# A depthwise convolution's product slots, laid token by token instead of slot by slot

## The chip, the cores and the metric

The kernel runs on one core of a Trainium2 chip. The metric is the device time of one execution in microseconds (us). The core's engines work side by side, each through a queue of its own in order: TensorE (PE; its weight loads are PEld), VectorE (DVE), ScalarE (ACT), GpSimd (POOL) and SyncE (SP, which issues the loads of weights).

## What is computed

The reference is a small decoder of two layers over 256 tokens of 2048 features: a Conformer convolution, an MLP, one shared K and V, an attention layer, a second MLP and a final norm. The change touches only the convolution of the first layer:

```python
def conformer_conv(y, w_in, b_in, w_dw, b_dw, ln_g, ln_b, w_out, b_out):
    u = y @ w_in + b_in
    a, gate = jnp.split(u, 2, axis=-1)
    u = a * jax.nn.sigmoid(gate)
    u = lax.conv_general_dilated(
        u, w_dw[:, None, :], window_strides=(1,), padding=[(CONV_WIDTH - 1, 0)],
        dimension_numbers=("NWC", "WIO", "NWC"), feature_group_count=u.shape[-1]) + b_dw
    u = jax.nn.silu(layernorm(u, ln_g, ln_b))
    return u @ w_out + b_out
```

The convolution is depthwise: each of the 2048 features has 31 taps of its own, and an output token is the sum of 31 products of a tap with an earlier token of the same feature.

## The kernel before

Activations lie with features on the 128 partitions and the 256 tokens along the free dimension, so 2048 features are 16 feature tiles, c = 0 to 15. Weights come in chunks of 1 MB (`raw`). Nearly every chunk is split into `hi` (a cast on ScalarE, L138) and `lo` (a subtraction, L140, on GpSimd for the chunks of this stage and on VectorE later), and a product runs as three matmuls per K tile (L193 to L195), 48 for a chunk. Eight chunks of the first product run unsplit as plain float32 (L199).

The stage of the change is a loop over the feature tiles. For tile c, TensorE makes the two halves `pa` and `pg` of the first product; ScalarE makes the sigmoid (L396), and VectorE multiplies both into `u` (L397), a tile of 30 zeros and 256 tokens, of which there are two in turn. Then `conv(c, u)` does the 31 taps:

- ScalarE makes 14 products, each the 256 tokens from a shifted start times one tap per partition (L303), into slots of two `prod` tiles of 8 slots by 256 tokens, float32, three buffers in turn.
- GpSimd adds one slot to another in the first tile and two to two in the second (L311), which frees three slots; ScalarE refills them with the last three of its 14 products.
- VectorE makes two running sums over the other 17 taps in PSUM (L324, L327, L329). Their last steps write slots 0 and 1 of the first `prod` tile.
- VectorE reduces the 8 slots of the first tile into slot 0 of the second (L335, 2048 words to 256), and the 6 slots of the second into the result `v` (L335, 1536 words to 256).

Tile 15 differs: TensorE takes 18 of its taps as products with diagonals (made on ScalarE at L413 during tile 11), and there is one reduction only. A slot is 256 contiguous words, so that the slots of one token lie 256 words, 1 KiB, apart. A tile's mean enters TensorE two tiles later (L418). From tile 12 on VectorE subtracts a provisional mean (L361) and ScalarE squares (L363); when all tiles are done, the LayerNorm's statistics follow and the second product begins.

The order on each engine is set by a scheduler that takes the program's order and priorities (`u` and its sigmoid have a high one) and estimates of its own, so edits can move instructions.

Of the kernel before, what the change touches and what calls it, by code (L numbers as in the profile page):

```python
# [11 lines left out]
F32 = mybir.dt.float32  # L12
# [9 lines left out]
KT = D // P          # feature tiles of the residual stream  # L22
# [7 lines left out]
FQ = 4               # quarters of the MLP's hidden layer  # L30
# [4 lines left out]
# Columns of the packed per-feature vectors: 16 feature tiles each.  # L35
# [5 lines left out]
LOOK = 4             # weight chunks split ahead of the one in use  # L41
RAWS = 3             # weight chunks on their way or waiting to be split
N0 = 4               # output tiles of a product that starts while its operand is still being made
LAST = 13            # K tiles before this one run for all of those

# The first mixer. Its products and its depthwise convolution keep every engine busy, so:
S1_PLAIN = {0, 1, 2, 3, 4, 5, 11, 28}   # chunks of its first product that run as float32
POOL_LO = (set(range(36)) - {28}) | set(range(183, 202, 2))   # chunks (here and in the attention) that GpSimd splits
SLOTS = 8            # partial sums of the convolution that one reduction adds up
# Per reduction: taps that ScalarE multiplies, and how many of them GpSimd adds to others, which makes  # L50
# room for as many more.
PIECES = [(6, 1), (5, 2)]
PE_TAPS = {15: (18, [(6, 1)])}   # feature tiles with taps on the tensor engine: how many, and their PIECES
DIAGS = {11: [15]}   # during which tile those taps' diagonals are made
Y_SPLIT = {0: 2, 1: 9, 2: 16}   # operand tiles that are split by the end of a feature tile
SHIFT = 10           # feature tiles whose mean is the LayerNorm's provisional one
CENTER = {12: [0, 3, 7], 13: [1, 2, 5, 6], 14: [4, 12, 13], 15: [8, 9, 10, 11, 14, 15]}   # when tiles are centered
AHEAD = {13: 31, 14: 34, 15: 34}   # chunks split after a feature tile's gate, where not the next tiles'
# [3 lines left out]
def decoder_kernel(ctx, tc, xT, vec, rope, mask, w_in, w_out, w_k, w_v, w_q, w_o, m_in, m_out, out):  # L62
    """Activations lie feature-major: tile k of a [2048, 256] activation holds features
    128k..128k+127 on the partitions and the 256 tokens along the free dimension. A weight chunk
    [128, 16, 128] holds all of K for 128 output features, so one PSUM tile [128, 256] accumulates
    over its 16 K tiles.

    float32 products: both operands are split exactly, v = hi + lo, hi = v rounded to float32r's 12
    significant bits and lo = v - hi (which has 12 at most), and x.w = xh.wh + xl.wh + xh.wl, each an
    exact one-pass product that is summed in float32. What is left, xl.wl, is below float32's last  # L70
    place of x.w. Attention's own products and a part of the first one, where the vector engine is
    short of time, run as plain float32.
    """
# [30 lines left out]
    def load():  # L104
        """Load as many chunks as there is room for. Those that are not split take a split one's place."""
        while len(raws) < min(len(order), n_used[0] + LOOK + RAWS):
            i = len(raws)
            src, split = order[i]
            if live[split] == ROOM[split]:
                break  # L110
            live[split] += 1
            raw = wp.tile([P, D], F32, name="raw", tag="w")
            if i == 0:
                for j in range(2):
                    nc.sync.dma_start(out=raw[:, j * D // 2:(j + 1) * D // 2], in_=src[:, j * D // 2:(j + 1) * D // 2])
                    nc.sync.dma_start(out=h[:, 4 * j + 4:4 * j + 8, :], in_=xT[:, 4 * j + 4:4 * j + 8, :])
            else:
                nc.sync.dma_start(out=raw, in_=src)
            raws.append(raw)
# [5 lines left out]
    def split_upto(n):  # L125
        """Make the chunks before the n-th ready for use."""
# [60 lines left out]
    def product(ps, w, acts, ks):  # L187
        """ps += the chunk's 128 output features over the K tiles ks."""
# [19 lines left out]
    def scaled_split(f, gain):  # L208
        """hi and lo of tile f of the residual stream times a gain vector."""
# [8 lines left out]
    def col_sums(st, s, first, last):  # L218
        """st[:, b] += a feature tile's part of the mean over features, tokens of half b on the partitions."""
# [9 lines left out]
    def spread(pb, rc):  # L229
        """A per-token column [128, 2] along every partition: [128, 256]."""  # L230
# [3 lines left out]
    class Rms:  # L234
        """The inverse root mean square per token of the residual stream, from tiles as they come."""
# [13 lines left out]
        def columns(self):  # L249
            """[tokens of a half, half]"""  # L250
# [8 lines left out]
        def rows(self):  # L259
            """The same along every partition."""  # L260
# [7 lines left out]
    with ExitStack() as s1:  # L268
# [16 lines left out]
        def conv(c, u):  # L285
            """Depthwise convolution: VectorE's two running sums and ScalarE's products (some added up by
            GpSimd), added up in reductions; the tensor engine may take taps as products with a diagonal."""
# [12 lines left out]
            def scaled(buf, slots):  # L300
                nonlocal j
                for i in slots:
                    nc.scalar.activation(out=buf[:, i, :], in_=u[:, j:j + T], func=AF.Copy, scale=tap(c, j))  # L303
                    j += 1

            for n, m in pieces:
                buf = prodp.tile([P, SLOTS, T], F32, name="prod")
                scaled(buf, range(carry, carry + n))
                if m:
                    room = slice(carry + m, carry + 2 * m)  # L310
                    nc.gpsimd.tensor_tensor(out=buf[:, carry:carry + m, :], in0=buf[:, carry:carry + m, :],  # L311
                                            in1=buf[:, room, :], op=ALU.add)
# [5 lines left out]
            # The running sums are in PSUM: with both inputs in SBUF, VectorE would shut GpSimd out of it.  # L318
            last = bufs[0][0]
            for i, j in enumerate(range(j, TAPS)):  # L320
# [7 lines left out]
                else:  # L328
                    nc.vector.scalar_tensor_tensor(out=a if j < TAPS - 2 else last[:, i % 2, :], in0=x,  # L329
# [3 lines left out]
            for i, (buf, n) in enumerate(bufs):  # L333
                dst = bufs[i + 1][0][:, 0, :] if i + 1 < len(bufs) else v_of(c)
                nc.vector.tensor_reduce(out=dst, in_=buf[:, :n, :].rearrange("p j t -> p t j"), axis=AX.X, op=ALU.add)  # L335
# [23 lines left out]
        def center(c):  # L359
            """Take the provisional mean from tile c, and square it."""  # L360
# [5 lines left out]
        def statistics():  # L366
            """Add the tiles centered so far to the statistics. (What the provisional mean leaves of the
            tiles that it is of sums to nothing.)"""
# [57 lines left out]
        # LayerNorm over the channels. With v less the provisional mean, the mean that is left has a  # L426
        # square of at most (KT - SHIFT) / KT of the mean square, so the difference is a safe variance.
# [52 lines left out]
    def project(acts, add, gain, steps, last):  # L480
        """The first N0 output tiles run together, K tile by K tile as the steps give them (a step may
        also be a function to call), because the operand is still being made. The K tiles from last on
        go output tile by output tile, so that the next chunk need not wait for all of them."""
# [71 lines left out]
    def rotate(src):  # L555
        """Rotary embedding of the first 32 rows of a [128, 256] head, in place."""
# [43 lines left out]

# [1 line left out]
    # The three branches see subsets of the causal keys with the same scores, and are mixed by the  # L602
    # softmax of their log-sum-exps: that is one softmax in which a key counts as often as branches
    # see it. The mask holds the logarithm of that count. Heads go in pairs that share K and V.
# [3 lines left out]
    def scores(p):  # L608
        """Scores and softmax of a pair: queries on the partitions, keys along the free dimension."""
# [29 lines left out]
    def flip(p):  # L639
        """Softmax weights with the keys on the partitions."""  # L640
# [12 lines left out]
    def mix(p):  # L653
        """The pair's outputs, feature-major and split."""
# [53 lines left out]
def rope_rows():  # L708
    """[32, 2, 256]: cosines and signed sines of the rotated rows, by position."""
# [6 lines left out]
def branch_counts():  # L716
    """[128, 2, 256]: for query 128b+p and each key, the log of how many branches see it."""
# [10 lines left out]
def chunks(w):  # L728
    """[K, N] -> [N/128, 128, K/128 * 128]: for each tile of output features, K by partition."""
# [38 lines left out]
```

## Time and profile before

| what | value |
|---|---|
| time, median of 3 runs | 2118.87 us (2116.08 to 2118.92) |
| span of the profiled execution | 2114.3 us |
| TensorE, busy share of the span | 97% |
| VectorE, busy share | 59% |
| ScalarE, busy share | 45% |
| GpSimd, busy share | 10% |

The span runs from the first to the last instruction of one profiled execution; the measured time also holds what lies around it. Busy shares are averages over stages with different limits. A releaser is what ended an engine's idle time.

### The profile page before, as it was taken

To read this page: it belongs to the slowest core of one execution; us is meant where nothing else is said; L and a number is where in the kernel's file an instruction comes from. 1 tells how busy PE (TensorE), PEld (TensorE's weight loads), DVE (VectorE), ACT (ScalarE), POOL (GpSimd) and SP (SyncE) were. 2 spreads that over 40 slices of the span, in tenths; PEclk is the share of its full clock that TensorE was granted. 3 is DMA by queue.
4 is the path that set the end of the run, shared out by engine and by line. 5 is a ranking of instruction groups with operands and counts; after the bars stand their busy time and mean duration, and the time that the engine had idled before them with its cause. 6 is when DMAs were issued, how large, how long until landed. Compare 5 with 4: busy or idle time off the path is not lost.

```text
span 2114.3 us, 37655 instructions
## 1 busy us (share of the span) xinstructions
PE 2058.0 (97%) x16630; PEld 2032.8 (96%) x16630; DVE 1256.0 (59%) x1499; ACT 955.6 (45%) x1192; POOL 213.0 (10%) x83
## 2 busy tenths in 40 slices
PE   8989799999999999999999999999999999999997
PEld 7888799999999999999999889999999999999997
DVE  7999975554554455445565876555455445545553
ACT  4677664443343344344453554444344334434442
POOL 2687500000000000000003220000000000000000
PEclk9999899999999999999999999999999999999999
DMA  7344235555555555555444334555455545555552
GB/s 285 140 146 153 102 127 186 181 188 182 180 182 188 188 180 180 184 189 186 180 180 179 140 140 149 190 180 180 180 183 189 187 179 181 184 190 184 180 181 79
DMA packets 51619, 368.01 MB, mean 174 GB/s; under 512 B 5856, under 2 KB 5856, under 8 KB 7552
## 3 DMA queue, kind: packets, MB, share of 16 engines
q1 hardware_dynamic: 51312, 365.60, 48.1%
q8 instruction: 130, 2.13, 0.4%
q14 instruction: 33, 0.27, 0.0%
q10 hardware_dynamic: 144, 0.01, 0.0%
HBM read 363.49 MB, written 2.10 MB: 173 GB/s over the span
## 4 chain that ended last, share of the span: by engine, by line
PE 49%; issue 36%; DVE 12%; ACT 2%; POOL 0%; POOLq 0%; DVEq 0%; ACTq 0%
PE ps L193 16%; PE ps L194 15%; PE ps L195 15%; DVE ps L329 3%; DVE prod L335 2%; DVE act L335 2%; DVE sh L559 1%; ACT hi L138 1%; ACT prod L303 1%; DVE prod L329 1%; DVE act L361 0%; PE ps L620 0%; PE ps L593 0%; PE ps L591 0%; PE ps L592 0%
## 5 line engine op out<-in xcount | busy, mean ns | idle before, releaser
L193 PE MATMUL ps<-act,hi 128*128 128x256 f32 x5312 | 1507.5, 284 | 2.7 <-ACT act L205 2.7
L195 PE MATMUL ps<-act,lo 128*128 128x256 f32 x5312 | 1502.2, 283 | 3.0 <-DVE lo L140 3.0
L194 PE MATMUL ps<-act,hi 128*128 128x256 f32 x5312 | 1501.6, 283 | 0.0
L138 ACT CAST hi<-raw 128x2048 fp32r<-128x2048 f32 x336 | 640.0, 1905 | 948.8 <-PE ps L194 791.6
L194 PEld LDWEIGHTS ps<-act,hi 128*128 128x128 f32 x5312 | 1018.0, 192 | 0.6
L195 PEld LDWEIGHTS ps<-act,lo 128*128 128x128 f32 x5312 | 1014.2, 191 | 3.7 <-DVE lo L140 3.4
L193 PEld LDWEIGHTS ps<-act,hi 128*128 128x128 f32 x5312 | 1013.3, 191 | 3.9 <-ACT act L205 3.1
L140 DVE TENSOR_TENSOR lo<-raw,hi 128x2048 fp32r<-128x2048 f32 x298 | 682.9, 2292 | 395.9 <-ACT hi L138 395.8
L477 DVE TENSOR_TENSOR h<-ps,h 128x256 f32<-128x256 f32 x144 | 61.0, 424 | 214.0 <-PE ps L195 213.8
L140 POOL TENSOR_TENSOR lo<-raw,hi 128x2048 fp32r<-128x2048 f32 x38 | 175.0, 4609 | 126.5 <-ACT hi L138 66.3
L226 POOL TENSOR_TENSOR rc<-ms,neg_half 128x2 f32<-128x2 f32 x5 | 3.6, 729 | 1703.4 <-DVE ms L255 1703.4
L516 DVE SCALAR_TENSOR_TENSOR t<-ps,t 128x256 f32<-128x256 f32 x128 | 54.2, 425 | 161.5 <-PE ps L195 161.5
L303 ACT ACTIVATE prod<-u,vecs 128x256 f32<-128x256 f32 x217 | 90.5, 497 | 58.0 <-DVE u L397 53.8
L329 DVE SCALAR_TENSOR_TENSOR ps<-u,vecs,ps 128x256 f32<-128x256 f32 x197 | 79.6, 483 | 0.0
L199 PE MATMUL ps<-act,raw 128*128 128x256 f32 x256 | 59.4, 393 | 6.5 <-DVE act L280 6.5
L199 PEld LDWEIGHTS ps<-act,raw 128*128 128x128 f32 x256 | 50.3, 198 | 13.7 <-DVE act L280 6.5
L206 DVE TENSOR_TENSOR act<-t,act 128x256 fp32r<-128x256 f32 x144 | 60.3, 420 | 0.9 <-ACT act L205 0.9
L205 ACT CAST act<-t 128x256 fp32r<-128x256 f32 x144 | 58.6, 407 | 4.5
L335 DVE TENSOR_REDUCE prod<-prod 128x256 f32<-128x2048 f32 x15 | 58.1, 3873 | 1.6 <-ACT prod L303 0.5
L518 ACT ACTIVATE t<-t 128x256 f32<-128x256 f32 x128 | 52.7, 412 | 4.8 <-DVE t L516 4.8
L335 DVE TENSOR_REDUCE act<-prod 128x256 f32<-128x1536 f32 (+1 forms) x16 | 47.0, 2939 | 0.4
L243 ACT ACTIVATE t<-h 128x256 f32<-128x256 f32 x80 | 31.5, 407 | 28.2 <-DVE h L477 22.2
(103 smaller groups left out, 600.9 us busy)
## 6 DMA issues: line engine op xcount, KB each, us to landing
raw<-in_m_in SPq DMA_DIRECT2D x128, 1024.0 KB, 4.8
raw<-in_m_out SPq DMA_DIRECT2D x128, 1024.0 KB, 4.8
raw<-in_w_in SPq DMA_DIRECT2D x31, 1024.0 KB, 4.9
raw<-in_w_out SPq DMA_DIRECT2D x16, 1024.0 KB, 4.9
raw<-in_w_q SPq DMA_DIRECT2D x16, 1024.0 KB, 4.8
raw<-in_w_o SPq DMA_DIRECT2D x16, 1024.0 KB, 4.8
raw<-in_w_k SPq DMA_DIRECT2D x4, 1024.0 KB, 5.1
raw<-in_w_v SPq DMA_DIRECT2D x4, 1024.0 KB, 4.9
```

What stands on the lines that cost most here:

```text
L138: nc.scalar.copy(out=hi, in_=raw)
L140: eng.tensor_tensor(out=lo, in0=raw, in1=hi.bitcast(F32), op=ALU.subtract)
L193: nc.tensor.matmul(ps, lhsT=wh, rhs=a[:, 0, :], start=k == 0, stop=False)
L194: nc.tensor.matmul(ps, lhsT=wh, rhs=a[:, 1, :], start=False, stop=False)
L195: nc.tensor.matmul(ps, lhsT=wl, rhs=a[:, 0, :], start=False, stop=k == KT - 1)
L199: nc.tensor.matmul(ps, lhsT=w[:, k * P:(k + 1) * P], rhs=act_of(k), start=k == 0, stop=k == KT - 1)
L205: nc.scalar.copy(out=a[:, 0, :], in_=src)
L206: nc.vector.tensor_tensor(out=a[:, 1, :], in0=src, in1=a[:, 0, :].bitcast(F32), op=ALU.subtract)
L303: nc.scalar.activation(out=buf[:, i, :], in_=u[:, j:j + T], func=AF.Copy, scale=tap(c, j))
L329: nc.vector.scalar_tensor_tensor(out=a if j < TAPS - 2 else last[:, i % 2, :], in0=x, scalar=tap(c, j), in1=a, op0=ALU.mult, op1=ALU.add)
L335: nc.vector.tensor_reduce(out=dst, in_=buf[:, :n, :].rearrange("p j t -> p t j"), axis=AX.X, op=ALU.add)
L477: nc.vector.tensor_tensor(out=h[:, f, :], in0=ps, in1=h[:, f, :], op=ALU.add)
```

## The change

A `prod` tile becomes 256 tokens by 8 slots instead of 8 slots by 256 tokens. Everything that writes or reads a slot follows: ScalarE's products, the two last running sums, both operands and the result of GpSimd's adds, and slot 0 of the second tile, to which the first reduction writes, now step 8 words (32 bytes) from token to token. The reductions now read each token's slots side by side. Number and size of the instructions stay as they are, and so does the order of the additions. The rest of the diff removes comments.

```diff
-                    nc.scalar.activation(out=buf[:, i, :], in_=u[:, j:j + T], func=AF.Copy, scale=tap(c, j))
+                    nc.scalar.activation(out=buf[:, :, i], in_=u[:, j:j + T], func=AF.Copy, scale=tap(c, j))
...
-                buf = prodp.tile([P, SLOTS, T], F32, name="prod")
+                buf = prodp.tile([P, T, SLOTS], F32, name="prod")
...
-                    nc.gpsimd.tensor_tensor(out=buf[:, carry:carry + m, :], in0=buf[:, carry:carry + m, :],
-                                            in1=buf[:, room, :], op=ALU.add)
+                    nc.gpsimd.tensor_tensor(out=buf[:, :, carry:carry + m], in0=buf[:, :, carry:carry + m],
+                                            in1=buf[:, :, room], op=ALU.add)
...
-                    nc.vector.scalar_tensor_tensor(out=a if j < TAPS - 2 else last[:, i % 2, :], in0=x,
+                    nc.vector.scalar_tensor_tensor(out=a if j < TAPS - 2 else last[:, :, i % 2], in0=x,
...
-                dst = bufs[i + 1][0][:, 0, :] if i + 1 < len(bufs) else v_of(c)
-                nc.vector.tensor_reduce(out=dst, in_=buf[:, :n, :].rearrange("p j t -> p t j"), axis=AX.X, op=ALU.add)
+                dst = bufs[i + 1][0][:, :, 0] if i + 1 < len(bufs) else v_of(c)
+                nc.vector.tensor_reduce(out=dst, in_=buf[:, :, :n], axis=AX.X, op=ALU.add)
```

The scheduler moves a few instructions. ScalarE, in a tile from the middle of the stage, with what each row waits for (`Pool` is GpSimd's add, `DMAHW` a chunk's arrival; - is before, + is changed):

```order
 L303 ACTIVATE prod<-u_114,vecs 128x256 x4
-L138 CAST hi<-raw 128x2048 [waits DMAHW1_49,PE_49]
-L303 ACTIVATE prod<-u_114,vecs 128x256 [waits Pool_49] x2
+L303 ACTIVATE prod<-u_114,vecs 128x256 [waits Pool_49]
+L138 CAST hi<-raw 128x2048 [waits DMAHW1_49,PE_49]
+L303 ACTIVATE prod<-u_114,vecs 128x256 [waits Pool_49]
 L303 ACTIVATE prod<-u_114,vecs 128x256 [waits Activation_49]
 L396 ACTIVATE t<-ps,vecs 128x256 [waits PE_49]
```

The first refill product has gone ahead of the weight cast. GpSimd in the middle tiles, before:

```order
L140 TENSOR_TENSOR lo<-raw,hi 128x2048 x2
L311 TENSOR_TENSOR prod<-prod 128x256
L311 TENSOR_TENSOR prod<-prod 128x512
L140 TENSOR_TENSOR lo<-raw,hi 128x2048 x2
L311 TENSOR_TENSOR prod<-prod 128x256
L311 TENSOR_TENSOR prod<-prod 128x512
```

And the same tiles in the changed kernel:

```order
L140 TENSOR_TENSOR lo<-raw,hi 128x2048
L311 TENSOR_TENSOR prod<-prod 128x256
L140 TENSOR_TENSOR lo<-raw,hi 128x2048
L311 TENSOR_TENSOR prod<-prod 128x256x2
L140 TENSOR_TENSOR lo<-raw,hi 128x2048
L311 TENSOR_TENSOR prod<-prod 128x256
L140 TENSOR_TENSOR lo<-raw,hi 128x2048
L311 TENSOR_TENSOR prod<-prod 128x256x2
```

One of a tile's two weight splits now stands between its two adds. SyncE's queue stays the same. In the last tiles some steps of VectorE and ScalarE change places, by one or two instructions.

## Rows read from the trace of the kernel before

**Rows 1.** The page: busy time of TensorE; busy tenths of VectorE, 40 slices.

```profile
PE 2058.0 (97%) x16630; PEld 2032.8 (96%) x16630; DVE 1256.0 (59%) x1499; ACT 955.6 (45%) x1192; POOL 213.0 (10%) x83
...
DVE  7999975554554455445565876555455445545553
```

**Rows 2.** Busy time by stretch: length, engines with instruction counts, clock, DMA share, GB/s.

```profile
120.00:140.00 20.00, 16.61 (x133) 16.10 (x133) 19.90 (x32) 15.79 (x30) 14.72 (x8) 1.00 0.44 159
140.00:160.00 20.00, 18.30 (x151) 18.04 (x151) 19.79 (x28) 12.43 (x21) 17.25 (x6) 1.00 0.43 153
...
240.00:260.00 20.00, 15.64 (x62) 14.10 (x63) 20.00 (x26) 11.31 (x24) 9.25 (x4) 0.66 0.27 102
...
320.00:340.00 20.00, 20.00 (x169) 20.00 (x169) 12.68 (x15) 7.87 (x9) 0.00 (x0) 1.00 0.48 164
```

**Rows 3.** The chain that ended last, 0 to 400 us, shares by line.

```profile
by line: DVE ps L329 16.7%; DVE prod L335 12.6%; DVE act L335 11.6%; PE ps L193 10.6%; PE ps L195 10.5%; PE ps L194 10.4%; issue 2.7%; ACT prod L303 2.7%; DVE prod L329 2.7%; DVE act L361 2.3%; DVE act L206 1.7%; ACT hi L138 1.4%; DVE ps L3
```

**Rows 4.** Timeline of VectorE, one feature tile: start us, us, instruction.

```profile
132.97 2.91 DVE L335 TENSOR_REDUCE act<-prod 128x256 f32<-128x1536 f32 x1
135.78 0.55 DVE L324 TENSOR_SCALAR ps<-u,vecs 128x256 f32<-128x256 f32 x1
...
136.61 5.20 DVE L329 SCALAR_TENSOR_TENSOR ps<-u,vecs,ps 128x256 f32<-128x256 f32 x13
141.70 0.88 DVE L329 SCALAR_TENSOR_TENSOR prod<-u,vecs,ps 128x256 f32<-128x256 f32 x2
142.69 3.90 DVE L335 TENSOR_REDUCE prod<-prod 128x256 f32<-128x2048 f32 x1
146.49 0.49 DVE L397 SCALAR_TENSOR_TENSOR u<-ps,vecs,t 128x256 f32<-128x256 f32 x1
146.88 2.90 DVE L335 TENSOR_REDUCE act<-prod 128x256 f32<-128x1536 f32 x1
```

**Rows 5.** Timeline of ScalarE, the same tile; in brackets idle time before, and its releaser.

```profile
133.09 4.50 ACT L303 ACTIVATE prod<-u,vecs 128x256 f32<-128x256 f32 x11 [4.21 <-DVE u L397]
137.50 1.90 ACT L138 CAST hi<-raw 128x2048 fp32r<-128x2048 f32 x1
139.29 1.30 ACT L303 ACTIVATE prod<-u,vecs 128x256 f32<-128x256 f32 x3
140.50 0.46 ACT L396 ACTIVATE t<-ps,vecs 128x256 f32<-128x256 f32 x1
140.86 1.89 ACT L138 CAST hi<-raw 128x2048 fp32r<-128x2048 f32 x1
```

**Rows 6.** Timeline of GpSimd, the same tile.

```profile
134.94 0.73 POOL L311 TENSOR_TENSOR prod<-prod 128x256 f32<-128x256 f32 x1
137.27 1.30 POOL L311 TENSOR_TENSOR prod<-prod 128x512 f32<-128x512 f32 x1 [1.60 <-ACT prod L303]
139.53 9.34 POOL L140 TENSOR_TENSOR lo<-raw,hi 128x2048 fp32r<-128x2048 f32 x2 [0.96 <-POOL prod L311]
```

**Rows 7.** Groups by line and shape, 0 to 330 us: busy us, mean ns; idle before.

```profile
L303 ACT ACTIVATE prod<-u,vecs 128x256 f32<-128x256 f32 x217 | 90.5, 497 | 58.0 <-DVE u L397 53.8 <-POOL prod L311 2.8 <-DVE prod L335 1.5
...
L335 DVE TENSOR_REDUCE prod<-prod 128x256 f32<-128x2048 f32 x15 | 58.1, 3873 | 1.6 <-ACT prod L303 0.5
...
L335 DVE TENSOR_REDUCE act<-prod 128x256 f32<-128x1536 f32 x15 | 43.4, 2890 | 0.4
```

**Rows 8.** Groups by line and shape, whole span: the reductions of attention, over contiguous rows.

```profile
L626 DVE TENSOR_REDUCE mx<-act 128x2 f32<-128x512 f32 x8 | 5.3, 666 | 0.0
...
L626 DVE TENSOR_REDUCE mx<-act 128x2 f32<-128x256 f32 x8 | 3.2, 401 | 0.0
```

**Rows 9.** ScalarE in 14 stretches of the stage, their sum; its longest wait.

```profile
sum 223.35, ACT 158.97; mean ACT 11.36
...
ACT prod L303 <- DVE u L397: 53.8, 15, 7.2
```

**Rows 10.** Timeline of VectorE: the last tile's reduction.

```profile
257.65 3.68 DVE L335 TENSOR_REDUCE act<-prod 128x256 f32<-128x2048 f32 x1
```

## The prediction

> **What bounds the kernel now.** I read the page first: over the whole span the tensor engine is busy 97% of the time, so most of the kernel is bound by its products, and a change to the convolution can only matter where something else sets the pace. The slices show where that is: the vector engine stands at 9 tenths only in the first five slices, which is the first mixer, and at 4 to 6 afterwards [rows 1]. Next come the 20 us stretches: between 120 and 160 us VectorE is busy 19.8 to 19.9 us of 20 while TensorE does 133 or 151 matmuls, against 169 in a stretch where only products run [rows 2]. The chain that ended last agrees. Up to 400 us its largest entries are three lines of the convolution on VectorE: the running sums (L329) and the two reductions (L335) [rows 3].
>
> Then one feature tile in detail. The second reductions of two neighbouring tiles start at 132.97 and 146.88, so a tile takes 13.91 us, and VectorE has no gap in it [rows 4]. ScalarE works in the same tile on 14 tap products, two weight casts and a sigmoid, and then stands still for 4.21 us until VectorE delivers the next u [rows 5]: 13.91 - 4.21 = 9.70 us of work. GpSimd has two adds (0.73 and 1.30 us) and two weight splits (9.33 us together), 11.36 us [rows 6]. TensorE needs 96 matmuls at 20 / 169 = 0.118 us, 11.4 us [rows 2], and something for the statistics. So VectorE is first at 13.9, and the others are not far behind.
>
> **The reductions get shorter.** They read slots that lie 1 KiB apart: 3.873 us for 2048 words and 2.890 us for 1536 [rows 7]. The trace has the same operation on contiguous rows, in attention: 666 ns for 512 words and 401 ns for 256 [rows 8]. That is 265 / 256 = 1.035 ns a word and 136 ns fixed. At this price the first reduction takes 2.256 us and the second 1.726 us: 1.617 + 1.164 = 2.78 us less in each of 15 tiles, 41.7 us, and 1.4 us in the last tile, whose single reduction takes 3.68 us [rows 10]. In all 43 us of VectorE's time, nearly all of which is now on the path. That the first reduction now writes with a stride costs nothing that I can see: it writes 256 words while it reads 2048.
>
> **The writes get a stride, and have no row of their own.** 217 products of ScalarE, 32 last running sums of VectorE and 31 adds of GpSimd now write (GpSimd also reads) words that are 32 bytes apart. No instruction before does that, so I bound it. Below: nothing, since a stride gives an engine no less to write, so a gain is excluded. Above, the nearest row is the reduction's own read: (3.873 - 0.136) / 2048 = 1.825 ns a word where contiguous words take 1.035, so 0.79 ns extra on average. This average has two readings. If each word that doesn't lie beside the one just accessed pays the same, a strided write pays 0.79 ns too: 0.202 us for 256 words. But that read comes back: eight words later it takes the neighbours of the eight it has just read. If the second word of such a pair is cheap, the first pays 2 x 0.79 = 1.58 ns, and the new writes, which never come back to a neighbour within an instruction, pay it on each word: 0.405 us for 256. I take the upper value, because the new pattern lacks the very thing that could have made the old one mild, and I keep 0 and 0.202 for the range. That ScalarE pays per word what VectorE pays is an assumption: I put the price down to the memory, which both share.
>
> [...]
>
> **What it costs by engine, a tile.** VectorE: 13.91 - 2.78, plus two strided running sums at 0.405: 11.9 us. GpSimd: its add goes from 0.73 to 1.30 us when it doubles, so 768 words a tile; with an extra of 0.79 ns on one stream at the least and 1.58 ns on both reads at the most, 0.6 to 2.4 us, it comes to 12.0 to 13.8 us. ScalarE: 9.70 + 14 x 0.405 = 15.4 us. So ScalarE would take VectorE's place, and above the old 13.91. The point from which it decides is its idle time, 4.21 / 14 = 0.301 us a product.
>
> **The sum over the stage.** From ScalarE's first product to its last table load the stretches add up to 223.35 us, of which ScalarE works 158.97 [rows 9]. 217 x 0.405 = 87.9 us more make 246.9 us, 23.5 us more than there is room for, if ScalarE no longer waits. It need not: its wait for u, 53.8 us over 15 tiles [rows 9], ends because VectorE would now be early, and the weight cast behind the sigmoid (1.89 us [rows 5]) covers the 0.49 us in which u is made [rows 4]. Behind the last product comes one reduction, 1.4 us shorter. Net +22.1 us.
>
> **What moves.** The refill product that needs GpSimd's first add goes ahead of a weight cast on ScalarE. That add ends at 135.7 [rows 6], the place of the product is at 137.5 [rows 5], so nothing waits; if it did, the cast, GpSimd's split of it and then TensorE would be held up. On GpSimd one split now stands between the two adds. The second add needs the tenth product, at 15.4 us a tile some 8 us after the first starts, and the split takes 4.6 us: at nothing. At a price of zero for the strides, it would hold the last refills back by up to 3 us, within ScalarE's 4.21 us. SyncE's queue doesn't move.
>
> The profiled execution has a span of 2114.3 us; the median of the three runs, 2118.87 us, is 4.6 us over it, and I take that as what lies around it. 2114.3 + 4.6 + 22.1 = 2141 us.
>
> **The rivals.**
> *The mild price (0.79 ns a word).* ScalarE comes to 9.70 + 14 x 0.202 = 12.5 us a tile, GpSimd to 12.0 to 12.6, VectorE to 11.5. Over the stage ScalarE needs 158.97 + 43.8 = 202.8 of 223.35 us, so at most 20.6 us can be saved; less some 4.8 us that it waits for u in the first tiles, where operand splits lie ahead of u on VectorE, -16 us: 2103 us. For it: it is the plain average of the only strided row. Against it: that row returns to neighbours. [...]
> *Writes cost nothing.* Then VectorE is at 11.1 us a tile, GpSimd at 11.4 if its reads cost nothing too, TensorE with its statistics near 12. The tile falls by 1.9 us in about 12 tiles, 23 us, and in the last three, where TensorE is mostly done (62 matmuls in 240 to 260 us [rows 2]), by all of 2.78: -31 us, 2088 us. For it: only reads with a stride are shown to be slow. Against it: nothing says that a write has more room than a read.
> *In between.* A price near 0.3 us a product fills ScalarE's gap and no more: within 4 us of before, 2119 us. It needs the price to fall in a narrow band.
> *The reduction doesn't get shorter*, because it is slow for another reason than its stride. The contiguous rows speak against it [rows 8]. Then the strides only cost: by the forecast's ledger 2142 us, by the mild price about 2120.
>
> **How the numbers follow.** Forecast, the high price with ScalarE as the bound: 0.45. Mild price: 0.27. No price: 0.18. In between: 0.08. Reduction unchanged: 0.02. A measurement of this kernel tells about 0.2%, 4 us, from no change. Slower: 0.45 + 0.02 = 0.47; the same: 0.08; faster: 0.27 + 0.18 = 0.45. Cases of both signs are strong, so the likeliest one's own range is 2125 (0.33 us a product: 158.97 + 71.6 - 223.35 - 1.4 = +6) to 2152 (0.45 us: +32). The range for 8 in 10 runs from 2095, which takes in the mild price and leaves most of the no-price case out, to 2152.
>
> **What would show it.** The reductions on L335 at 2.26 and 1.73 us, contiguous: the first step. L303 at 0.497 + 0.405 = 0.90 us on ScalarE: the second; at 0.70 the mild rival, at 0.50 the free one. ScalarE's wait for u near nothing, VectorE waiting for prod instead, a tile of 15.4 us, and the adds on GpSimd at up to 1.5 and 2.9 us: the third. The forecast is wrong if L303 comes out under 0.80 us, or if ScalarE still waits for u.

## The result, and the profile after

The changed kernel takes 2097.86 us, median of 4 runs (2096.33 to 2098.26), against 2117.49 us for the kernel before in the same set of runs: a ratio of 0.9907, with a 95% interval of 0.9893 to 0.9921. It is 19.6 us faster, where 22 us slower had been forecast. The profiled execution has a span of 2095.9 us, 18.4 us shorter than before.

Nearly all of it lies in the stage of the convolution: the copy that opens the LayerNorm's statistics (L430) starts 18.57 us earlier. Before, and in the changed kernel:

```profile
263.52 0.16 DVE L430 COPY mu<-ps 128x2 f32<-128x2 f32 x1 [1.21 <-PE ps L221]
```

```profile
244.95 0.16 DVE L430 COPY mu<-ps 128x2 f32<-128x2 f32 x1 [1.24 <-PE ps L221]
```

These are the changed kernel's groups by line and shape up to 310 us, with busy us, mean ns of one, and the idle time before them; they answer to [rows 7]:

```profile
L303 ACT ACTIVATE prod<-u,vecs 128x256 f32<-128x256 f32 x217 | 122.7, 760 | 17.6 <-DVE u L397 16.1 <-POOL prod L311 1.4
...
L335 DVE TENSOR_REDUCE prod<-prod 128x256 f32<-128x2048 f32 x15 | 34.3, 2287 | 3.4 <-ACT prod L303 2.4
L335 DVE TENSOR_REDUCE act<-prod 128x256 f32<-128x1536 f32 x15 | 26.2, 1744 | 0.4
L361 DVE TENSOR_TENSOR act<-act,shift 128x256 f32<-128x256 f32 x16 | 20.8, 1345 | 0.1
...
L329 DVE SCALAR_TENSOR_TENSOR prod<-u,vecs,ps 128x256 f32<-128x256 f32 x32 | 20.1, 703 | 0.1
L311 POOL TENSOR_TENSOR prod<-prod 128x512 f32<-128x512 f32 x15 | 20.1, 1341 | 14.8 <-ACT prod L303 11.5 <-PE ps L195 3.4
...
L206 DVE TENSOR_TENSOR act<-act 128x256 fp32r<-128x256 f32 x16 | 9.8, 677 | 0.0
```

Three groups of the kernel before, from the same view, that the rows ahead of the prediction don't have:

```profile
L329 DVE SCALAR_TENSOR_TENSOR prod<-u,vecs,ps 128x256 f32<-128x256 f32 x32 | 14.1, 474 | 0.0
...
L361 DVE TENSOR_TENSOR act<-act,shift 128x256 f32<-128x256 f32 x16 | 9.9, 664 | 0.0
...
L206 DVE TENSOR_TENSOR act<-act 128x256 fp32r<-128x256 f32 x16 | 7.2, 512 | 0.0
```

Read together, they are the account of VectorE's busy time. The reductions give back 42.4 us (58.1 + 43.4 and the last one's 3.7 before; 34.3 + 26.2 + 2.3 after). Strided running sums take 6.0 us of that, the centerings of the LayerNorm (L361) 10.9 us, the operand splits of the first tiles (L206) 2.6 us. That leaves 22.9 us; some 4.5 us more go into waits of VectorE that were not there. The centerings and splits are no part of the change: why they got longer is one of the questions below.

One feature tile of the changed kernel on VectorE (start us, us, instruction); it answers to [rows 4]:

```profile
133.39 1.74 DVE L335 TENSOR_REDUCE act<-prod 128x256 f32<-128x1536 f32 x1
...
135.89 5.18 DVE L329 SCALAR_TENSOR_TENSOR ps<-u,vecs,ps 128x256 f32<-128x256 f32 x13
140.98 1.23 DVE L329 SCALAR_TENSOR_TENSOR prod<-u,vecs,ps 128x256 f32<-128x256 f32 x2
142.31 2.29 DVE L335 TENSOR_REDUCE prod<-prod 128x256 f32<-128x2048 f32 x1
144.51 0.48 DVE L397 SCALAR_TENSOR_TENSOR u<-ps,vecs,t 128x256 f32<-128x256 f32 x1
144.90 1.74 DVE L335 TENSOR_REDUCE act<-prod 128x256 f32<-128x1536 f32 x1
```

and on ScalarE, which answers to [rows 5]:

```profile
133.51 6.62 ACT L303 ACTIVATE prod<-u,vecs 128x256 f32<-128x256 f32 x12
139.90 1.96 ACT L138 CAST hi<-raw 128x2048 fp32r<-128x2048 f32 x1
141.75 1.35 ACT L303 ACTIVATE prod<-u,vecs 128x256 f32<-128x256 f32 x2
142.83 0.48 ACT L396 ACTIVATE t<-ps,vecs 128x256 f32<-128x256 f32 x1
143.17 1.95 ACT L138 CAST hi<-raw 128x2048 fp32r<-128x2048 f32 x1
145.02 6.60 ACT L303 ACTIVATE prod<-u,vecs 128x256 f32<-128x256 f32 x12
```

A tile takes 144.90 - 133.39 = 11.51 us instead of 13.91. VectorE has no gap in it, as before. ScalarE has none either: in this tile its wait for u is gone, and yet it doesn't make the tile longer. The reason stands in the first two rows. Twelve products start at 133.51 and the cast behind them at 139.90, so a product starts 6.39 / 12 = 0.53 us after the one before, although each lasts 0.76 us: a product is still running for 0.23 us when the next one starts. Before, eleven took 137.50 - 133.09 = 4.41 us, 0.40 us each, at a duration of 0.50. So the stride made a product 0.263 us longer and put the next one 0.13 us off.

The stretch from 120 to 140 us (columns as in [rows 2]) shows a tile in which four engines are full:

```profile
120.00:140.00 20.00, 20.00 (x166) 19.89 (x165) 19.90 (x36) 20.00 (x33) 19.72 (x7) 1.00 0.47 169
```

TensorE does 166 matmuls in 20 us, where it did 133 and 151, and 169 where only products run [rows 2].

### The profile page after: what moved, and what is told of

It reads as the page before. It is cut to its first block, busy times and chain, and to the rows that moved or that the text cites. A ratio compares the mean times of both kernels' runs of the same rounds, so it can differ in the third digit from the quotient of the medians.

```text
span 2095.9 us, 37656 instructions
## 1 busy us (share of the span) xinstructions
PE 2054.7 (98%) x16630; PEld 2031.1 (97%) x16630; DVE 1232.9 (59%) x1499; ACT 983.9 (47%) x1192; POOL 211.4 (10%) x83
## 4 chain that ended last, share of the span: by engine, by line
PE 50%; issue 36%; DVE 9%; ACT 3%; POOL 1%; POOLq 0%; DVEq 0%; ACTq 0%
PE ps L193 16%; PE ps L194 16%; PE ps L195 16%; DVE ps L329 2%; ACT prod L303 1%; DVE sh L559 1%; ACT hi L138 1%; DVE prod L335 1%; DVE act L361 1%; DVE act L335 1%; PE ps L221 1%; PE ps L294 0%; DVE act L206 0%; POOL lo L140 0%; PE ps L620 0%
## 5 line engine op out<-in xcount | busy, mean ns | idle before, releaser
L303 ACT ACTIVATE prod<-u,vecs 128x256 f32<-128x256 f32 x217 | 122.7, 760 | 17.6 <-DVE u L397 16.1
L206 DVE TENSOR_TENSOR act<-t,act 128x256 fp32r<-128x256 f32 x144 | 60.3, 420 | 1.0 <-ACT act L205 1.0
L335 DVE TENSOR_REDUCE prod<-prod 128x256 f32<-128x2048 f32 x15 | 34.3, 2287 | 3.4 <-ACT prod L303 2.4
L311 POOL TENSOR_TENSOR prod<-prod 128x256 f32<-128x256 f32 (+1 forms) x31 | 31.7, 1024 | 38.5 <-ACT prod L303 28.7
```

The lines of the kernel that those rows point to most:

```text
L206: nc.vector.tensor_tensor(out=a[:, 1, :], in0=src, in1=a[:, 0, :].bitcast(F32), op=ALU.subtract)
L303: nc.scalar.activation(out=buf[:, :, i], in_=u[:, j:j + T], func=AF.Copy, scale=tap(c, j))
L335: nc.vector.tensor_reduce(out=dst, in_=buf[:, :, :n], axis=AX.X, op=ALU.add)
```

## The experiments

Two questions were open. What does a strided write cost, and whom? And why did VectorE's other instructions get longer? The kernel before ran again beside these runs, with medians of 2117.05 and 2118.87 us; the changed kernel did not. So a difference to the changed kernel is known to about 2 us.

**The reductions alone.** The slots stay as they were, the reductions read contiguous words:

```diff
-                nc.vector.tensor_reduce(out=dst, in_=buf[:, :n, :].rearrange("p j t -> p t j"), axis=AX.X, op=ALU.add)
+                nc.vector.tensor_reduce(out=dst, in_=buf[:, :n, :].rearrange("p j t -> p (j t)").rearrange("p (t j) -> p t j", j=n),
+                                        axis=AX.X, op=ALU.add)
```

> Slots stay slot by slot as before, so that every write is contiguous, but the reductions read the tile as one contiguous run (they add up the wrong words; all else is the same). Theory H (a strided write of 256 words takes ScalarE 0.263 us longer, but more than half of that runs beside the start of the next product, so it pays 0.12 us; the changed tile of 11.5 us is one at which TensorE, VectorE, ScalarE and GpSimd are all full): without strides ScalarE falls to 9.7 us a tile and VectorE to 11.1, but TensorE stays near 11.4, so the tile stays at 11.2 to 11.5 us and the kernel comes out 0 to 6 us under the changed one. Rival S (the strides are what holds the changed kernel back, as the forecast had it): the tile falls well under 11.4 us and the kernel gains 10 us or more on the changed one.

2087.7 us, ratio to before 0.9856 (0.9841 to 0.9871): 10.2 us under the changed kernel. The time is theory S's. The second reductions of this kernel, two tiles running, and its centerings:

```profile
128.79 1.74 DVE L335 TENSOR_REDUCE act<-prod 128x256 f32<-128x1536 f32 x1
...
139.94 1.75 DVE L335 TENSOR_REDUCE act<-prod 128x256 f32<-128x1536 f32 x1
```

```profile
L362 DVE TENSOR_TENSOR act<-act,shift 128x256 f32<-128x256 f32 x16 | 15.4, 1007 | 0.0
```

A tile takes 11.15 us, VectorE's own work without the strided sums. Theory H was wrong in that TensorE does not stand at 11.4 us: it fits into 11.15. And the centerings are 5.4 us shorter (20.8 to 15.4 us), with which the strides have nothing to do directly. So the strides, with what came after them, cost the changed kernel some 10 us. In VectorE's busy time that is 6.0 us of its own sums and 5.4 us of centerings that ran at another moment; how much of the time each of the two is worth, this run alone does not tell.

**The strided writes alone.** The reductions read words 1 KiB apart again, from a tile that is written with a stride (8 words in the first slot tile, 6 in the second):

```diff
-                buf = prodp.tile([P, T, SLOTS], F32, name="prod")
+                buf = prodp.tile([P, T * SLOTS], F32, name="prod")
+                buf = buf[:, :T * (carry + n)].rearrange("p (t j) -> p t j", j=carry + n)
...
-                nc.vector.tensor_reduce(out=dst, in_=buf[:, :, :n], axis=AX.X, op=ALU.add)
+                nc.vector.tensor_reduce(out=dst, in_=buf.rearrange("p t j -> p (t j)").rearrange("p (j t) -> p t j", j=n), axis=AX.X,
+                                        op=ALU.add)
```

> Products, adds and last running sums write with a stride as in the changed kernel (8 words for the first slot tile, 6 for the second), and the reductions read words 1 KiB apart as before (they add up the wrong words). Theory H: ScalarE comes to 11.4 us a tile, under VectorE's 13.9, so only VectorE's own two strided sums count, 2 x 0.23 us a tile, and its tile goes to 14.2 to 14.4 us: 3 to 8 us slower than before. The forecast's price (0.405 us a product): ScalarE at 15.4 us a tile, 20 us or more slower. Price of the duration (0.263 us): ScalarE at 13.4 us, as theory H.

2128.3 us, ratio 1.0049 (1.0032 to 1.0065), 9.4 us slower, a little beyond theory H's 3 to 8 and far from the forecast's 20 and more. The first reductions of two neighbouring tiles, and ScalarE between them:

```profile
119.05 3.93 DVE L336 TENSOR_REDUCE prod<-prod 128x256 f32<-128x2048 f32 x1
...
133.47 3.96 DVE L336 TENSOR_REDUCE prod<-prod 128x256 f32<-128x2048 f32 x1
```

```profile
123.40 6.52 ACT L303 ACTIVATE prod<-u,vecs 128x256 f32<-128x256 f32 x12 [2.89 <-DVE u L399]
...
137.85 6.50 ACT L303 ACTIVATE prod<-u,vecs 128x256 f32<-128x256 f32 x12 [2.98 <-DVE u L399]
```

A tile takes 14.42 us, half a microsecond more than before, and ScalarE still stands 2.9 us of it waiting for u (4.2 before). At the forecast's price it would have been the bound at 15.4 us. The strided products are paid from its idle time: 14.42 - 2.94 = 11.48 us of work instead of 9.70 is 0.13 us for each of 14 products, the distance read above. What is seen in the time is VectorE's.

**Half a product at a time.** Each product in two instructions of 128 tokens:

```diff
-                    nc.scalar.activation(out=buf[:, :, i], in_=u[:, j:j + T], func=AF.Copy, scale=tap(c, j))
+                    for t in range(0, T, T // 2):
+                        nc.scalar.activation(out=buf[:, t:t + T // 2, i], in_=u[:, j + t:j + t + T // 2], func=AF.Copy,
+                                             scale=tap(c, j))
```

> The changed kernel with each of ScalarE's products made in two halves of 128 tokens, 28 instructions a tile instead of 14. Asked is only how far the starts of two neighbouring products lie apart. Theory H (a strided write goes on beside the start of the next product, and only what it takes beyond that counts): 128 words at 2.08 ns take 0.27 us, which hides wholly, so the distance is that of contiguous 128-word products, 0.29 to 0.31 us. Rival (each strided word costs 0.48 ns more, and nothing hides): 0.36 us.

ScalarE in this kernel, and its first reductions in two neighbouring tiles:

```profile
125.20 6.73 ACT L304 ACTIVATE prod<-u,vecs 128x128 f32<-128x128 f32 x22
131.68 1.97 ACT L138 CAST hi<-raw 128x2048 fp32r<-128x2048 f32 x1
```

```profile
122.72 2.28 DVE L337 TENSOR_REDUCE prod<-prod 128x256 f32<-128x2048 f32 x1
...
135.02 2.28 DVE L337 TENSOR_REDUCE prod<-prod 128x256 f32<-128x2048 f32 x1
```

The starts lie (131.68 - 125.20) / 22 = 0.295 us apart: theory H's distance, not the rival's 0.36. What contiguous products of 128 words take, the diagonals in the changed kernel show:

```profile
168.28 1.90 ACT L413 ACTIVATE act<-ident,vecs 128x128 f32<-128x128 f32 x6
170.03 6.11 ACT L303 ACTIVATE prod<-u,vecs 128x256 f32<-128x256 f32 x11
```

They start (170.03 - 168.28) / 6 = 0.292 us apart. With 128 words the stride costs ScalarE's queue nothing that shows. The kernel also shows the forecast's mechanism at work where the load is really there: 28 x 0.295 us of products, two casts and a sigmoid come to 12.2 us, more than VectorE's 11.5, and the tile takes 12.30 us, the kernel 2104.8 us in one run.

**A step of 64 bytes.** Tokens t and t+128 side by side, so that a product steps 16 words:

```diff
+            Q = 2
+
+            def slot(buf, i):
+                return buf.rearrange("p (t q) s -> p q t s", q=Q)[:, :, :, i]
...
-                    nc.scalar.activation(out=buf[:, :, i], in_=u[:, j:j + T], func=AF.Copy, scale=tap(c, j))
+                    nc.scalar.activation(out=slot(buf, i), in_=u[:, j:j + T].rearrange("p (q t) -> p q t", q=Q), func=AF.Copy, scale=tap(c, j))
```

> The changed kernel with a slot tile in which tokens t and t+128 lie side by side, so that a product steps 16 words (64 bytes) in two runs of 128 instead of 8 words in one of 256; the reductions still read one contiguous run. If a neighbourless write has one price whatever the step, products stay at 0.75 to 0.78 us and 0.53 us from start to start. If the price grows with the step, they come out above 0.85 us; if it falls with it, under 0.70.

```profile
L308 ACT ACTIVATE prod<-u,vecs 128x256 f32<-128x256 f32 x217 | 117.9, 716 | 19.6 <-DVE u L404 17.9 <-POOL prod L316 1.6
```

Products last 716 ns and lie 0.51 us apart (twelve from 121.36 us to the cast at 127.49), and one run takes 2098.65 us, as the changed kernel. The 716 ns fall between the expectations: below the band for one price, and just above the 0.70 us under which the price would fall with the step. So the price does not grow from 32 to 64 bytes; whether it falls a little is open, because the row was also cut into two runs, which is not told apart from the step here.

**Slots in pairs.** Two slots of a token side by side, four such pairs 2 KiB apart:

```diff
-                    nc.scalar.activation(out=buf[:, :, i], in_=u[:, j:j + T], func=AF.Copy, scale=tap(c, j))
+                    nc.scalar.activation(out=buf[:, i // 2, :, i % 2], in_=u[:, j:j + T], func=AF.Copy, scale=tap(c, j))
...
-                buf = prodp.tile([P, T, SLOTS], F32, name="prod")
+                buf = prodp.tile([P, SLOTS // 2, T, 2], F32, name="prod")
...
-                nc.vector.tensor_reduce(out=dst, in_=buf[:, :, :n], axis=AX.X, op=ALU.add)
+                nc.vector.tensor_reduce(out=dst, in_=buf[:, :n // 2].rearrange("p g t s -> p t g s"), axis=AX.XY,
+                                        op=ALU.add)
```

> Slots in pairs: a token's slots 2g and 2g+1 lie side by side, the four pairs 2 KiB apart, so products step 2 words instead of 8, and the reductions read pairs; GpSimd's second add takes the third pair onto the second (contiguous), and its refills go there. Theory N (what costs is a neighbourless access: a pair on 8 bytes is enough): reductions as short as in the changed kernel, 2.26 to 2.30 and 1.73 to 1.75 us, and products at 0.50 us or little more instead of 0.76. Rival (any step costs a write): products stay at 0.76 us. Time: TensorE's 11.4 us a tile remain, so 0 to 6 us under the changed kernel if N, the same if not.

2089.9 us, ratio 0.9865 (0.9851 to 0.988), 8 us under the changed kernel, a little more than the 0 to 6 expected, and nearly as fast as without any stride. Its groups:

```profile
L303 ACT ACTIVATE prod<-u,vecs 128x256 f32<-128x256 f32 x217 | 92.7, 516 | 29.5 <-DVE u L398 22.6 <-POOL prod L312 6.6
L335 DVE TENSOR_REDUCE prod<-prod 128x256 f32<-128x2048 f32 x15 | 34.3, 2285 | 1.6 <-ACT prod L303 0.5
L329 DVE SCALAR_TENSOR_TENSOR prod<-u,vecs,ps 128x256 f32<-128x256 f32 x32 | 14.1, 476 | 0.1
```

and one tile's products, with the cast behind them:

```profile
117.87 4.56 ACT L303 ACTIVATE prod<-u,vecs 128x256 f32<-128x256 f32 x11 [0.40 <-DVE u L398]
122.33 1.89 ACT L138 CAST hi<-raw 128x2048 fp32r<-128x2048 f32 x1
```

Theory N's figures come true: a product takes 516 ns instead of 497 and starts (122.33 - 117.87) / 11 = 0.41 us after the one before, VectorE's last sums take 476 ns instead of 474, and a reduction that reads pairs and then hops 2 KiB is as short as one over contiguous words (2285 ns against 2287). So the reductions agree with theory N. The writes, however, are no pairs: a product fills every second word, so it has no neighbour within the instruction either. Theory N's reason is therefore not what the writes show. What they show is that a step of 8 bytes cost 0.019 us on ScalarE and 0.002 us on VectorE, where 32 bytes cost 0.263 us on ScalarE and 0.229 us on VectorE for 256 words. The run with the strided writes alone has 24 bytes in its second slot tile, and its products last 745 ns on average over both, nearly as the 760 ns with 32 throughout; steps between 8 and 24 bytes were not tried.

**The centerings.** In the changed kernel ten of them stand in a row. VectorE there, and GpSimd at the same time:

```profile
168.60 9.80 DVE L361 TENSOR_TENSOR act<-act,shift 128x256 f32<-128x256 f32 x10
```

```profile
164.40 9.43 POOL L140 TENSOR_TENSOR lo<-raw,hi 128x2048 fp32r<-128x2048 f32 x2 [0.94 <-ACT hi L138]
173.77 0.90 POOL L311 TENSOR_TENSOR prod<-prod 128x256 f32<-128x256 f32 x1
```

The ten did not slow down evenly. The second of them, and the split beside it:

```profile
169.24 4.86 DVE L361 TENSOR_TENSOR act<-act,shift 128x256 f32<-128x256 f32 x1
```

```profile
169.00 4.82 POOL L140 TENSOR_TENSOR lo<-raw,hi 128x2048 fp32r<-128x2048 f32 x1
```

It started after the split and ended 174.10 - 173.82 = 0.28 us after it: it stood through the whole split. Eight of the 16 centerings met a split or an add of GpSimd that had started before them, and each ended 0.27 to 0.28 us after that instruction; the other eight took 0.41 to 0.43 us. The operand splits of the first tiles (L206) show the same. The changed kernel and the kernel before each have one that met a split of GpSimd, and both ended 0.28 us after it: 4.65 us in the changed kernel, 2.01 before. This difference is the 2.6 us of the account above.

In the kernel before, the same ten took 3.43 us, and GpSimd, which had no split to do then, was held up instead: its one add, which started after the first four of them, took 2.93 us and ended 0.60 us after the tenth.

```profile
188.59 3.43 DVE L361 TENSOR_TENSOR act<-act,shift 128x256 f32<-128x256 f32 x10
```

```profile
189.69 2.93 POOL L311 TENSOR_TENSOR prod<-prod 128x256 f32<-128x256 f32 x1 [3.85 <-DVE act L361]
```

A centering reads two operands from SBUF, and so does a split. The experiment leaves one operand, the provisional mean, in PSUM:

```diff
-                shift = up.tile([P, T], F32, name="shift")
-                nc.scalar.activation(out=shift, in_=pmean[:, :T], func=AF.Copy, scale=KT / SHIFT)
+                shift = pmean[:, :T]
+                nc.scalar.activation(out=shift, in_=shift, func=AF.Copy, scale=KT / SHIFT)
```

> The changed kernel with the LayerNorm's provisional mean left in PSUM, where ScalarE scales it in place, so that the 16 centerings of VectorE (L361 in the changed kernel) have one input in SBUF instead of two. Theory G (GpSimd's weight splits, which read two inputs from SBUF, hold VectorE's instructions with two SBUF inputs back; in the changed kernel the ten centerings in a row meet two splits and take 9.8 us instead of 3.4): the 16 centerings fall from 20.8 to some 7 us and the kernel gains 6 to 12 us. Rival: that stretch is bound by TensorE or ScalarE anyway, and the kernel gains under 3 us.

2091.0 us, ratio 0.987 (0.9855 to 0.9884), 6.8 us under the changed kernel:

```profile
L361 DVE TENSOR_TENSOR act<-act,ps 128x256 f32<-128x256 f32 x16 | 5.7, 415 | 0.0
```

The centerings fall from 20.8 to 5.7 us, and theory G holds. The statistics start 10.1 us earlier than in the changed kernel:

```profile
234.89 0.16 DVE L430 COPY mu<-ps 128x2 f32<-128x2 f32 x1 [2.05 <-PE ps L221]
```

So 15 us of VectorE give 10 us of the stage and 7 us of time; why 3 us are lost behind the stage stays open. In the changed kernel the centering that started just after a split took 4.86 us, against 0.41 to 0.43 us for those that met nothing; with one operand in PSUM the 16 take 415 ns on average.

The same edit in the kernel before:

> The kernel before with the provisional mean left in PSUM, nothing else. Theory G: there the ten centerings met no split (3.4 us) and one single centering took 4.2 us, so some 4 us are to be had, 2114 to 2116 us: the loss to GpSimd is mostly one that the changed kernel took on by its new order. Rival: the edit gains as much here as in the changed kernel, 7 us, and has nothing to do with the change.

2115.7 us, ratio 0.9991 (0.9982 to 1.0001): no difference that this measurement can tell. Its centerings fall from 9.9 to 5.8 us, which is the one centering of 4.21 us that stood through a split before, and the statistics start 2.7 us earlier:

```profile
260.80 0.16 DVE L430 COPY mu<-ps 128x2 f32<-128x2 f32 x1 [1.88 <-PE ps L221]
```

The time lies where theory G put it, but a gain of 4 us isn't shown. In the stage the edit gains 10.1 us in the changed kernel and 2.7 in the kernel before, so most of what it gains there was lost with the change.

**Pairs, and the mean in PSUM.**

> Both edits that gained on the changed kernel at once: slots in pairs, and the provisional mean left in PSUM. Theory G (GpSimd's splits hold VectorE's instructions with two SBUF inputs back): in the paired kernel the 16 centerings still take 17.9 us; they fall to 6 us, and the kernel comes out 5 to 9 us under the paired one, at 2081 to 2085 us, faster than all others. Rival (the two edits take away the same time): within 3 us of 2090.

2083.55 us, ratio 0.9843 (0.9828 to 0.9857): 33.5 us under the kernel before and 14.3 under the changed one, the fastest of all. Alone they gave 8.0 and 6.8 us, so the two edits take away different losses.

## Why the prediction was wrong, step by step

**What bounds the stage, and what that leaves for the gain: right.** VectorE's tile set the pace, the reductions fell to 2.287 and 1.744 us (2.256 and 1.726 forecast), 42.4 us in all (43 forecast), and outside the stage next to nothing moved (18.57 us of the stage, 18.4 of the span).

**The price of a strided write: the step that failed.** The prediction took 0.405 us a product, the upper of two readings of the old reduction's row, and put it whole onto ScalarE's queue. Both were too much. A product lasts 0.263 us longer, 1.03 ns a word, which lies between the two readings (0.79 and 1.58 ns). And its start-to-start distance, the only thing that counts on a full queue, grows by 0.13 us alone. The row for that was there: before, products lasted 0.497 us and started 0.40 us apart [rows 5, 7], so part of each already ran beside the next. The sum took the work of today as the queue takes it (9.70 us, overlaps included) and added the lengthening of each product in full. With 0.13 us the same ledger gives 9.70 + 14 x 0.13 = 11.5 us for ScalarE, no more than VectorE's 13.91 - 2.78 + 0.34 = 11.47 (its two strided sums put off the next instruction by 0.34 us, 142.31 - 140.98 against 142.69 - 141.70 before [rows 4]), and the tile measured is 11.51. Over the stage 217 x 0.13 = 28 us fit easily into the 64 us that ScalarE had free. The run with the strided writes alone shows it apart: at 0.405 us ScalarE would have bound at 15.4 us, and it waits 2.9 us in a tile of 14.42. The prediction's own sign was met: L303 came out at 0.760 us, under 0.80. The reason given for the upper reading, that a write without a neighbour pays on each word, does not hold as it stands either: in the run with pairs such writes step 8 bytes and cost 0.02 us.

**The point from which it decides: right in kind.** The halved products put ScalarE at 12.2 us, and there it did set the tile, at 12.30 us.

**GpSimd's adds: wrong.** They were given 0.6 to 2.4 us more a tile. The add of two slots takes 1.34 us on average, and 1.30 in the middle tiles, as before [rows 6]:

```profile
140.38 1.30 POOL L311 TENSOR_TENSOR prod<-prod 128x512 f32<-128x512 f32 x1
```

With strided operands and a strided result it pays nothing that shows.

**The rivals.** The mild price gave 2103 us, the free writes 2088. The measured 2097.9 lies between. The kernel with contiguous writes and short reductions takes 2087.7 us, so the free case met the total, partly by luck: its middle tiles fell by 2.76 us (13.91 to 11.15) and not by 1.9, because TensorE needed less than the 12 us that it was given, and the late tiles with their centerings gave the surplus back. Of the 31 us that it promised the strides and what came with them took 10. The case in which the reductions stay long was given about 2120 us at the mild price. That leaves out VectorE's own strided sums; the run with the strided writes alone is nearly this case, and took 2128.3.

**What the prediction didn't see.** It gave VectorE's other instructions no term. The centerings, eight of which now stood behind an instruction of GpSimd, cost VectorE nearly twice the busy time of all strided sums (10.9 against 6.0 us). The forecast noted that instructions change places, looked at ScalarE and GpSimd, and asked only who waits by semaphore. The row that could have warned was in the trace of the kernel before: one centering of 4.21 us, where the others took 0.41 to 0.57.

```profile
195.72 4.21 DVE L361 TENSOR_TENSOR act<-act,shift 128x256 f32<-128x256 f32 x1
```

**Small slips that change nothing.** After the fifth slice VectorE stands at 3 to 8 tenths, not 4 to 6 [rows 1]. The 4.6 us taken as what lies around the span are 1.8 us of that, as the profiled run's own 2116.1 us shows, and else the difference between runs. The upper end of the range adds up to 2151 us, not 2152.

**Range and chances.** The range, 2095 to 2152 us, holds the result near its lower end. The sign of the likeliest case was wrong; faster had 0.45.

## What to carry to other kernels

Price an instruction on a full queue by the distance from its start to the next one's, and what is added to it by that distance too: a duration that overlaps the next start overstates the cost, here twofold (0.263 us against 0.13). This layout did not have to choose between contiguous reads and contiguous writes: with the slots in pairs the reads found two neighbours on 8 bytes, the writes stepped 8 bytes, and both took about as long as contiguous ones (a reduction 2285 ns against 2287, a product 516 ns against 497). When an edit shifts the phase of the engines, look for VectorE instructions with two SBUF operands that now fall beside GpSimd work, as the centerings did here (20.8 us for the 16 instead of 9.9), or take one of their operands from PSUM (5.7 us); and look at single instructions, since a mean, here 1345 ns, hides that one took 4.86 us while eight took 0.41 to 0.43.

## What was not expected of the hardware

- A strided write on ScalarE of 256 words (32 bytes apart) starts 0.53 us after the one before, where contiguous ones lie 0.40 us apart; of 128 words 0.295 us, against 0.292 for contiguous ones: at that length the stride put the next one off by 0.003 us. No length between these was tried.
- At 8 bytes and full length the stride cost little: 516 ns instead of 497 on ScalarE, 476 instead of 474 on VectorE.
- On VectorE a running sum of 256 words that writes 32 bytes from word to word took 703 ns instead of 474, 0.9 ns a word more; on GpSimd the strided add took as long as the contiguous one (1.30 us for 512 words in the middle tiles).
- Where GpSimd's work and VectorE's centerings, with two SBUF operands, met in these two traces, either side paid, and it was the one that came later: a centering that started 0.24 us after a split stood through it and took 4.86 us instead of 0.41, and an add of GpSimd that started within the row of ten centerings ended 0.60 us after the row, with 2.93 us instead of 0.73.
